# MoE expert slots without a token: their rows neither gathered nor stored, skipped by row numbers past a bound, and the result table filled with zeros earlier

## The chip, the cores and the metric

The kernel runs on one core of one Trainium2 chip. A core has a matrix engine (TensorE, PE in the profile, its weight loads PEld), a vector engine (DVE), a scalar engine (ACT), a general engine (GpSimd, POOL) and a sync engine (SP), which mostly issues transfers. Each engine works through its own instructions in order and waits on semaphores. SP, ACT and POOL each issue DMA transfers to queues of their own; 16 DMA engines carry them. The metric is the device time of one execution in microseconds.

## The reference, cut to what matters

One step of a one-layer decoder on 1088 tokens (1024 of a prompt, 64 of a sample group): a projection, an RWKV recurrence and a windowed attention, an output projection, a mixture of experts, a per-layer embedding and a last norm. The change lies in the mixture of experts:

```python
gsel = argmax(hf @ w_group + b_group)                  # one of 4 groups
tv, ti = top_k(elog[gsel], 2)                          # two of its 8 experts
tw = softmax(tv) * gw
for e in range(32):                                    # D = 1024, width of an expert 256
    out = (silu(hf @ w_gate[e]) * (hf @ w_up[e])) @ w_down[e]
    acc += comb[:, e, None] * out                      # comb is 0 but for the two chosen
```

Each token goes to two experts, so 1088 x 2 = 2176 rows are needed in all.

## The kernel before

The program has six phases. Phase 1 (to about 395 us) projects all tokens with `w_in`, one column tile `ct` at a time (25 of them), in 3 chunks of tokens, on PE; while it runs, SP writes its results to DRAM and copies the key and value caches. Phases 2 and 3 (to about 950 us) are the recurrence and the attention, phase 4 (to about 1079 us) is the output projection and the routing, phase 5 (to about 1420 us) the experts, phase 6 the embedding and the last norm.

Routing gives each of the 32 experts a list of `CAP` = 96 slots, 3072 in all. `idx[slot, expert]` is the number of the token in a slot; it comes out of a matrix product (`pidx`), so an empty slot holds 0, the number of token 0. `slot[token, 0..1]` is the row of a token's two results in the table `YE` (3072 x 1024 floats, in DRAM). With the reference's inputs no expert gets more than 96 tokens, so 2176 of the 3072 slots are used and 896 (29%) are empty.

Phase 5 does for each expert e:

- `gather(e)`: an indirect DMA on POOL's queue (L1532) fetches 96 rows of 4 KB from `HN` (the normed tokens) into `x5`. There are three buffers for x5, so gather e needs that PE is done with the x5 of expert e-3. It is asked for in round e-3.
- `xt(e)`: 8 PE transposes (L1542), and a split of the result in a high and a low part (ACT writes the high one, L47, DVE the low one, L49).
- `gu(e)`: 24 matmuls (128 x 512) with the gate and up weights, `act(e)` the gating, `ht(e)` two transposes.
- `down(e)`: 12 matmuls, evacuated by ACT in two halves into `y5` (L1575, three buffers, so y5 of expert e needs that the store of expert e-3 has landed), then a plain DMA on ACT's queue (L1576) that stores all 96 rows to rows 96e to 96e+95 of `YE`.

The weights of each expert (3.1 MB) are fetched by SP three rounds (gate, up) and five rounds (down) ahead, and split by ACT and DVE into high and low parts. In round 25 stands an `If` (L1647) on the largest count of an expert, with a path for full experts that isn't taken here. Phase 6 adds the two results of each token by indirect gathers of `YE` on POOL (L1712).

The order of the instructions of each engine isn't that of the source: a scheduler that keeps a simulated time line places them, all six phases together, so an edit in one place can move instructions elsewhere.

## Time and profile before

| | us |
|---|---|
| three runs | 1567.76, 1574.98, 1576.21 (median 1574.98) |
| the profiled execution | 1571.74 |
| its span, first to last instruction | 1570.0 |
| PE busy in the span | 1382.5 (88%) |
| DVE, ACT, POOL busy | 960.4, 738.1, 369.8 |
| experts, first transpose to last store's issue | 1079 to 1420 |

The busy shares are means over phases that are limited by different things. In the rows further down, a DMA share of 1.00 means that all 16 engines were busy all the time; values a little above come from the way in which packets are counted. "PEclk" is the clock granted to PE, 1.00 being full speed.

### The profile page before, as it was taken

How to read it: one execution, taken by the hardware profiler on the slowest of the kernel's cores; microseconds unless marked ns; L12 is line 12 of the kernel's file. 1: busy time of each engine (PE TensorE's matmuls, PEld its weight loads, DVE VectorE, ACT ScalarE, POOL GpSimd, SP SyncE). 2: the span in 40 equal slices, each digit the busy share in tenths (PEclk: the TensorE clock that was granted, in tenths of full speed). 3: DMA queues.
4: the chain of work that ended last, by engine and by line, in shares of the span. 5: the costliest groups of instructions: out<-in, count | busy, mean ns of one | idle time of the engine just before them, and what ended most of it. 6: DMA issues, size and time to landing. Idle time of an engine off the chain costs nothing. (4 is left out here: it accounts for less than half of the span.)

```text
span 1570.0 us, 24571 instructions
## 1 busy us (share of the span) xinstructions
PE 1382.5 (88%) x9017; PEld 1152.6 (73%) x9018; DVE 960.4 (61%) x2155; ACT 738.1 (47%) x1336; POOL 369.8 (24%) x362
## 2 busy tenths in 40 slices
PE   4899999999898998975679899995999789899996
PEld 4888999999777776754568678784777566567874
DVE  7524573462287686444457563567988678786664
ACT  5544453221334444522345463243878668783322
POOL 8104453000122223242122351112221101002231
PEclk9999999999898999987889899997999989999998
DMA  6145658896775675255586647558999999997552
GB/s 207 52 156 177 181 154 262 288 353 222 218 216 150 176 190 154 69 120 142 128 255 214 171 128 258 198 212 272 377 391 381 378 332 332 353 379 251 181 173 67
DMA packets 257005, 350.01 MB, mean 223 GB/s; under 512 B 105757, under 2 KB 184415, under 8 KB 256352
## 3 DMA queue, kind: packets, MB, share of 16 engines
q1 hardware_dynamic: 212272, 287.46, 56.0%
q0 software_dynamic: 39712, 43.76, 9.9%
q10 hardware_dynamic: 4896, 17.17, 2.9%
q8 instruction: 73, 1.20, 0.3%
q14 instruction: 52, 0.43, 0.1%
HBM read 277.45 MB, written 104.33 MB: 243 GB/s over the span
## 5 line engine op out<-in xcount | busy, mean ns | idle before, releaser
L264 PE MATMUL pj<-hT_hi,wh 128*128 128x384 f32 (+1 forms) x600 | 199.5, 334 | 4.7 <-DVE lora L272 2.7
L264 PE MATMUL pj<-hT_hi,wl 128*128 128x384 f32 (+1 forms) x600 | 199.1, 332 | 0.0
L264 PE MATMUL pj<-hT_lo,wh 128*128 128x384 f32 (+1 forms) x600 | 198.4, 331 | 0.0
L264 PEld LDWEIGHTS pj<-hT_hi,wh 128*128 128x128 f32 x600 | 114.0, 191 | 6.6 <-DVE lora L272 3.0
L264 PEld LDWEIGHTS pj<-hT_hi,wl 128*128 128x128 f32 x600 | 114.0, 190 | 2.4 <-issue 2.2
L264 PEld LDWEIGHTS pj<-hT_lo,wh 128*128 128x128 f32 x600 | 114.4, 191 | 0.6 <-issue 0.2
L1532 POOL DMA_INDIRECT x<-HN,idx x32 | 49.9, 1560 | 255.2 <-PE p4t L1542 154.1
L49 DVE TENSOR_TENSOR dl<-draw,dh 128x1024 fp32r<-128x1024 f32 x66 | 78.0, 1221 | 43.8 <-ACT dh L47 43.6
L1040 PE MATMUL pS<-k,q 128*128 128x512 f32 (+2 forms) x192 | 55.7, 397 | 37.9 <-DMA q<-QP 36.5
L688 DVE TENSOR_TENSOR ftmp<-At,X 128x60 f32<-128x60 f32 (+24 forms) x248 | 59.7, 252 | 44.1 <-DMA At<-ABd 33.5
L1069 PEld LDWEIGHTS po<-v,pt 128*128 128x128 f32 x576 | 74.5, 198 | 11.0 <-issue 2.7
L1069 PE MATMUL po<-v,pt 128*128 128x128 f32 x576 | 80.0, 284 | 1.6 <-ACT pt L1067 1.3
L1052 ACT ACTIVATE s<-s,nm 128x128 f32<-128x128 f32 (+7 forms) x64 | 49.4, 772 | 62.7 <-DVE X L744 21.5
L47 ACT ACTIVATE dh<-draw 128x1024 fp32r<-128x1024 f32 x66 | 66.2, 1052 | 22.9 <-DMA draw<-in_w_down_dram 13.5
L1040 PEld LDWEIGHTS pS<-k,q 128*128 128x128 f32 x192 | 32.2, 206 | 44.2 <-issue 31.9
L1043 DVE CUSTOM_DVE_ANT_0 s<-pS,bias 128x512 f32<-128x512 f32 (+2 forms) x96 | 50.8, 551 | 19.5 <-PE pxt L1063 15.9
L49 DVE TENSOR_TENSOR wl<-w,wh 128x1024 fp32r<-128x1024 f32 x25 | 35.0, 1400 | 44.6 <-ACT wh L47 43.8
L690 DVE TENSOR_TENSOR X<-X,ftmp 128x60 f32<-128x60 f32 (+24 forms) x248 | 58.7, 248 | 4.5
L1067 ACT ACTIVATE pt<-pxt 128x512 f32<-128x512 f32 (+3 forms) x64 | 32.6, 512 | 58.9 <-PE pxt L1063 44.1
L767 POOL TENSOR_TENSOR s<-S,pc 128x512 f32<-128x512 f32 x16 | 16.9, 1055 | 161.9 <-PE pj L264 70.6
L1289 PE MATMUL p4y<-dh,hh 128*96 128x512 f32 x128 | 46.9, 407 | 7.5 <-ACT hh L47 7.5
L1289 PE MATMUL p4y<-dh,hl 128*96 128x512 f32 x128 | 51.3, 401 | 1.3 <-DVE hl L49 1.3
(653 smaller groups left out, 3793.4 us busy)
## 6 DMA issues: line engine op xcount, KB each, us to landing
wraw<-in_w_gate_dram SPq DMA_DIRECT2D x64, 512.0 KB
wraw<-in_w_up_dram SPq DMA_DIRECT2D x64, 512.0 KB
draw<-in_w_down_dram SPq DMA_DIRECT2D x32, 1024.0 KB
out_dram<-in_cache_k_win_dram SPq DMA_DIRECT2D x16, 1016.0 KB
out_dram<-in_cache_v_win_dram SPq DMA_DIRECT2D x16, 1016.0 KB
w<-in_w_in_dram SPq DMA_DIRECT2D x25, 512.0 KB
kc<-in_cache_k_win_dram SPq DMA_DIRECT2D x48, 256.0 KB
vc<-in_cache_v_win_dram SPq DMA_DIRECT2D x48, 256.0 KB
```

Of the source, the lines that this page charges most:

```text
L47: (hi_eng or nc.scalar).activation(hi, src, AF.Copy) if (hi_eng or nc.scalar) is nc.scalar else hi_eng.tensor_copy(hi, src)
L49: return e.tensor_tensor(lo, src, hi.bitcast(F32), op=ALU.subtract)
L264: nc.tensor.matmul(p[:, :nn], a[:, k, :], b[:, k, n0:n0 + nn], start=(m == 0), stop=(m == 23))
L688: nc.vector.tensor_tensor(o, At[:, t, t + 1:32][:, :, None].to_broadcast([128, m, c]), X[:, t, None, 0:c].to_broadcast([128, m, c]), op=AL ...
L690: nc.vector.tensor_tensor(X[:, t + 1:32, 0:c], X[:, t + 1:32, 0:c], o, op=ALU.add)
L1040: nc.tensor.matmul(ps[:, :n], q[:, a, i * 128:(i + 1) * 128], k[:, c0:c0 + n], start=(a == 0), stop=(a == 1))
L1043: nc.vector.tensor_tensor_reduce(s[:, c0:c0 + n], ps[:, :n], bias[:, bo:bo + n], 1.0, -3e38, ALU.add, ALU.max, m)
L1052: ex = nc.scalar.activation(s[:, :nb * 128], s[:, :nb * 128], AF.Exp, bias=nm, accum_out=den)
L1067: nc.scalar.activation(pt[:, b0:b0 + m, :], px[:, :m, :], AF.Copy)
L1069: nc.tensor.matmul(po, pt[:, b, :], v[:, b, :], start=(b == 0), stop=(b == nb - 1))
L1289: self.nc.tensor.matmul(p, a[x][:, k, :], w, start=(k == 0 and q == 0), stop=(k == kn - 1 and q == 2))
L1532: nc.gpsimd.indirect_dma_start(out=X[e][:n], out_offset=None, in_=self.HN, in_offset=bass.IndirectOffsetOnAxis(ap=self.idx[:, e:e + 1], ax ...
```

## The change

`idx` gets 2048 added, and the table of token numbers from which it is made has 2048 taken off: a used slot holds its token's number as before, an empty one 2048. The gather gets a bound, the last token (1087): rows whose number is above are skipped. A second index `row[slot, expert]` holds the slot's row in `YE`, plus 4096 where the slot is empty. The store becomes an indirect DMA on POOL's queue with this index and the bound 3071, again with skipping. `YE` is filled with zeros in phase 1 by 12 DMAs of 1 MB on SP, one for each of the projections number 8 to 19 (`n`), each with a declared wait for the evacuation of that projection's first chunk.

```diff
@@ project
+            if n0 == 0 and 8 <= n < 20:
+                z = nc.sync.dma_start(self.YE[256 * (n - 8):256 * (n - 7), :].rearrange("(p a) (b c) -> p (a b) c", a=2, c=512),
+                                      self.S0.rearrange("p i v -> p (i v)")[:, None, :].to_broadcast([128, 4, 512]))
+                self.tc.add_manual_dep(z.ins, a.ins.name, ...)
@@ constants
+FREE = 2048
-    row[:, 140:149] = j[:, None] + 128 * np.array(ORD)[None, :]
+    row[:, 140:149] = j[:, None] + 128 * np.array(ORD)[None, :] - FREE
+    row[:, 149] = j
@@ phase4_
-        self.after_idx = nc.vector.tensor_copy(self.idx, pidx[:CAP, 0:NE])
+        nc.vector.tensor_scalar(self.idx, pidx[:CAP, 0:NE], float(FREE), None, op0=ALU.add)
+        free = p4.tile([CAP, NE], F32, name="free")
+        nc.vector.tensor_scalar(free, pidx[:CAP, 0:NE], 0.0, float(2 * FREE), op0=ALU.is_ge, op1=ALU.mult)
+        nc.vector.scalar_tensor_tensor(self.row, free, row[:CAP], ist[:CAP], op0=ALU.add, op1=ALU.add)
@@ gather
             nc.gpsimd.indirect_dma_start(out=X[e][:n], out_offset=None, in_=self.HN,
-                                         in_offset=bass.IndirectOffsetOnAxis(ap=self.idx[:, e:e + 1], axis=0))
+                                         in_offset=bass.IndirectOffsetOnAxis(ap=self.idx[:, e:e + 1], axis=0),
+                                         bounds_check=T - 1, oob_is_err=False)
@@ down
-            return nc.scalar.dma_start(self.YE[e * n:e * n + n, :], y[:n])
+            return nc.gpsimd.indirect_dma_start(out=self.YE, out_offset=bass.IndirectOffsetOnAxis(ap=self.row[:, e:e + 1], axis=0),
+                                                in_=y[:n], in_offset=None, bounds_check=NE * CAP - 1, oob_is_err=False)
```

Before, the stores of two experts write different rows by their addresses, and nothing orders them. An indirect store may write any row of `YE` as far as the program can tell, so each one waits until the one before it has landed, and the first `y6` gather of phase 6 waits for the last.

The order of instructions changes on every engine. On POOL, before, the gathers of phase 5 stand one behind the other (here those of experts 15 to 20; the number behind a name is its buffer's):

```order
L1532 DMA x5_12321<-HN_88,idx_9885 96x1024
L1532 DMA x5_12423<-HN_88,idx_9885 96x1024
L1532 DMA x5_12525<-HN_88,idx_9885 96x1024
L1532 DMA x5_12627<-HN_88,idx_9885 96x1024
L1532 DMA x5_12729<-HN_88,idx_9885 96x1024
```

Now, just ahead of the `If`, the gathers of experts 27 and 28 (x5_13661, x5_13767) and the stores of experts 14 to 24 (y5_12719 to y5_13779) stand like this:

```order
L1588 DMA YE_89<-y5_12719,row_9898 3072x1024
L1543 DMA x5_13661<-HN_88,idx_9897 96x1024
L1588 DMA YE_89<-y5_12825,row_9898 3072x1024
L1543 DMA x5_13767<-HN_88,idx_9897 96x1024
L1588 DMA YE_89<-y5_12931,row_9898 3072x1024
L1588 DMA YE_89<-y5_13037,row_9898 3072x1024
...
L1588 DMA YE_89<-y5_13673,row_9898 3072x1024
L1588 DMA YE_89<-y5_13779,row_9898 3072x1024
L1659 TENSOR_LOAD ci_13812
```

POOL has now 32 stores between its gathers. Behind gather 28 stand nine stores in a row (experts 16 to 24), behind the `If` gathers 29 and 30, store 25, gather 31, the stores 26 to 31, and then the first gather of phase 6.

On ACT, before, the two evacuations of expert 24 and its store's issue are all that stands of down in the stretch ahead of the `If`, with splits of weights between them:

```order
L1575 ACTIVATE y5_13657<-p4y_13658 96x512
L47 ACTIVATE dh_13679<-draw_13277 128x1024 x2
L1575 ACTIVATE y5_13657<-p4y_13666 96x512
L47 ACTIVATE wha_13653<-wraw_13486 128x1024
L47 ACTIVATE wha_13675<-wraw_13486 128x1024
L1576 DMA YE_89<-y5_13657 96x1024
L47 ACTIVATE whb_14208<-wraw_13585 128x1024
L47 ACTIVATE whb_14212<-wraw_13585 128x1024
L1646 TENSOR_LOAD ci_13688
```

Now the evacuations of experts 21 to 24 (y5_13461, y5_13567, y5_13673, y5_13779) come there close together:

```order
L1587 ACTIVATE y5_13461<-p4y_13470 96x512
L1587 ACTIVATE y5_13567<-p4y_13568 96x512
L47 ACTIVATE dh_13591<-draw_13173 128x1024 x2
L1587 ACTIVATE y5_13567<-p4y_13576 96x512
...
L1587 ACTIVATE y5_13673<-p4y_13674 96x512
L47 ACTIVATE dh_13697<-draw_13279 128x1024 x2
L1587 ACTIVATE y5_13673<-p4y_13682 96x512
...
L1587 ACTIVATE y5_13779<-p4y_13780 96x512
L47 ACTIVATE dh_13803<-draw_13385 128x1024 x2
L1587 ACTIVATE y5_13779<-p4y_13788 96x512
L1659 TENSOR_LOAD ci_13812
```

On PE the downs have moved likewise: from about expert 9 on they fall behind the gate and up products, to five experts behind (the down of expert 19 stands in the gate and up of expert 23), and those of 19 to 24 stand in the last rounds ahead of the `If`.

On SP, in phase 1, before, a row of cache copies, stores and weight loads:

```order
L596 DMA bb0_99<-BB_70 64x4x64 x4
L281 DMA out_8_dram<-in_cache_k_win_dram 16x16256
L281 DMA out_9_dram<-in_cache_v_win_dram 16x16256
L297 DMA QP_76<-qhi_2523 128x1024
L608 DMA AR_2216<-ARd_68 128x4x256
L608 DMA AR_2322<-ARd_68 128x4x256
```

Now the zero fills (L277) stand among them, two in this stretch:

```order
L600 DMA bb0_99<-BB_70 64x4x64 x4
L277 DMA YE_89<-S0_109 512x1x512
L285 DMA out_8_dram<-in_cache_k_win_dram 16x16256
L285 DMA out_9_dram<-in_cache_v_win_dram 16x16256
L612 DMA AR_2222<-ARd_68 128x4x256
L612 DMA AR_2328<-ARd_68 128x4x256
L301 DMA QP_76<-qhi_2530 128x1024
L301 DMA QP_76<-qlo_2531 128x1024
L302 DMA QT_78<-qk_2442 128x64
L277 DMA YE_89<-S0_109 512x1x512
L235 DMA w_2823<-in_w_in_dram 128x8x128
```

A weight load `w` that stands behind a zero fill is issued only after it.

## Rows read from the trace of the kernel before

**Rows 1.** The page: span, busy time of the engines, data rate in 40 slices.
```profile
span 1570.0 us, 24571 instructions
PE 1382.5 (88%) x9017; PEld 1152.6 (73%) x9018; DVE 960.4 (61%) x2155; ACT 738.1 (47%) x1336; POOL 369.8 (24%) x362
GB/s 207 52 156 177 181 154 262 288 353 222 218 216 150 176 190 154 69 120 142 128 255 214 171 128 258 198 212 272 377 391 381 378 332 332 353 379 251 181 173 67
```

**Rows 2.** Windows of phase 5: busy us of each engine, then PEclk, DMA share, GB/s.
```profile
core 0: us, PE busy (x) PEld busy (x) DVE busy (x) ACT busy (x) POOL busy (x), PEclk, DMA share, GB/s
1100.00:1166.00 66.00, 66.00 (x333) 47.35 (x332) 61.52 (x78) 55.20 (x82) 17.80 (x7) 1.00 1.03 382
1166.00:1318.00 152.00, 136.77 (x648) 94.93 (x647) 119.34 (x151) 111.23 (x166) 18.96 (x15) 0.94 0.99 356
1352.00:1424.00 72.00, 67.55 (x320) 48.55 (x318) 58.30 (x72) 54.45 (x80) 3.18 (x4) 0.96 0.88 333
```

**Rows 3.** Timeline of POOL, gathers of experts 9, 10, 14 and 28: start, us.
```profile
1121.39 2.86 POOL L1532 DMA_INDIRECT x<-HN,idx  x1 [6.29 <-PE p4t L1542]
1130.53 2.86 POOL L1532 DMA_INDIRECT x<-HN,idx  x1 [6.29 <-PE p4t L1542]
...
1166.64 0.91 POOL L1532 DMA_INDIRECT x<-HN,idx  x1 [7.63 <-PE p4t L1542]
...
1318.30 2.17 POOL L1532 DMA_INDIRECT x<-HN,idx  x1 [2.09 <-PE p4t L1542]
```

**Rows 4.** DMA queues, 1105 to 1225 us: packets, MB, share; gathers' landing.
```profile
q1 hardware_dynamic: 9696, 36.03, 77.8%
q0 software_dynamic: 1504, 5.31, 13.9%
q10 hardware_dynamic: 1456, 5.11, 10.7%
...
x<-HN,idx POOLq DMA_INDIRECT x14, 9.2
```

**Rows 5.** The same view, 960 to 1065 us: POOL's queue, stores to DRAM only.
```profile
q0 software_dynamic: 2096, 7.60, 18.5%
...
HN<-hn POOLq DMA_DIRECT2D x8, 512.0 KB, 6.8
X<-x POOLq DMA_DIRECT2D x7, 512.0 KB, 5.8
```

**Rows 6.** Tile x: all 32 gathers, ns min, median, max on POOL.
```profile
L1532 POOL DMA_INDIRECT x<-HN,idx x32: 905/1021/3158, 1072.6 to 1369.0; - x32
```

**Rows 7.** Timeline of the end of phase 5: last store, first gather of phase 6, its reader.
```profile
1420.13 0.31 ACTq L1576 DMA_DIRECT2D YE<-y  x1
...
1423.98 0.98 POOL L1712 DMA_INDIRECT y<-YE,slot  x1 [54.02 <-DMA PL<-ple]
...
1429.03 1.28 DVE L1721 SCALAR_TENSOR_TENSOR x<-y,wgt,x 128x1024 f32<-128x1024 f32 x1 [1.48 <-DMA y<-YE,slot]
...
1442.63 1.04 PE L1736 MATMUL p4t<-ident,hp 128*128 128x128 f32 x8
```

**Rows 8.** Phase 1: two windows, columns as in rows 2.
```profile
200.00:300.00 100.00, 98.55 (x621) 97.73 (x620) 46.76 (x44) 39.38 (x69) 31.50 (x23) 1.00 0.72 229
300.00:400.00 100.00, 97.31 (x608) 96.38 (x607) 45.49 (x157) 21.69 (x41) 0.88 (x2) 0.98 0.82 278
```

**Rows 9.** DMA queues, 200 to 260 us, then 260 to 330 us.
```profile
q1 hardware_dynamic: 17217, 10.81, 61.0%
...
q1 hardware_dynamic: 14481, 21.76, 90.0%
```

**Rows 10.** Timeline of the start of phase 5.
```profile
1071.53 0.17 DVE L1484 CAST idx<-p4g 96x32 int32<-96x32 f32 x1
...
1079.11 1.54 PE L1542 MATMUL p4t<-ident,x 96*128 96x96 f32 x8 [7.82 <-DMA x<-HN,idx]
```

More of the change, by code (lines that the diff above doesn't have):

```diff
@@ L271, in project @@
                     nc.scalar.activation(self.sh[:, :, ct], p[:, o:o + 65:8], AF.Copy)
-                nc.vector.scalar_tensor_tensor(out[:, n0:n0 + nn], p[:, :nn], self.omu[:, ct:ct + 1],
+                a = nc.vector.scalar_tensor_tensor(out[:, n0:n0 + nn], p[:, :nn], self.omu[:, ct:ct + 1],
                                                tmp[:, n0:n0 + nn], op0=ALU.mult, op1=ALU.add)
@@ L275, in project @@
                 a = nc.scalar.activation(out[:, n0:n0 + nn], p[:, :nn], AF.Copy, scale=0.125 if ct < 17 else 1.0)
+            if n0 == 0 and 8 <= n < 20:
+                z = nc.sync.dma_start(self.YE[256 * (n - 8):256 * (n - 7), :].rearrange("(p a) (b c) -> p (a b) c", a=2, c=512),
+                                      self.S0.rearrange("p i v -> p (i v)")[:, None, :].to_broadcast([128, 4, 512]))
+                self.tc.add_manual_dep(z.ins, a.ins.name, mybir.DependencyInfo(mybir.DependencyClass.Sync, mybir.DependencyReason.DATA))
         return a if ct >= 13 else None
@@ L1305, in phase4_ @@
         self.idx = c4.tile([CAP, NE], I32, name="idx")
+        self.row = c4.tile([CAP, NE], I32, name="row")
         xs_p = I['x_prompt'].rearrange("o t d -> (o t) d")
@@ L1315, in phase4_ @@
         i4, i8, ist = rc[:, 128:132], rc[:, 132:140], rc[:, 140:172]
-        irk, tid = rc[:, 172:172 + CAP], rc[:, 268:277]
+        irk, tid, row = rc[:, 172:172 + CAP], rc[:, 268:277], rc[:, 277:278]
         ones = p4.tile([128, 128], F16, name="ones")
```

## The prediction

> **What bounds the kernel now.** I read the page first, then cut the span into phases by windows, then asked in phase 5 for the pace of the experts and for the DMA queues. On the page PE is busy 88% of the span [rows 1], so one could take it for the bound everywhere; but the data rate reaches its highest values, 330 to 390 GB/s, in slices 29 to 36, which are phase 5. The windows of that phase [rows 2] show two regimes. From 1100 to 1166 us PE is busy all of the time while the DMA engines are full (1.03): weights are still ahead from phase 4. From 1166 to 1318 us PE is busy for 136.8 of 152 us, DVE for 119 and ACT for 111, and the DMA share stays at 0.99: nothing on the compute engines is full, the DMA engines are. The gathers of POOL give the pace, since one is asked for per expert [rows 3]: 9.14 us apart at 1121 to 1130 us, the pace of a full PE; from expert 14's at 1166.64 to expert 28's at 1318.30 it is 151.7 / 14 = 10.83 us per expert, the pace of the DMA engines. So bytes taken out of phase 5 are worth time for about 20 experts, down to a floor of PE's 9.14 us.
>
> **What a row costs.** In 1105 to 1225 us, 120 us, the queues' shares give the price of a MB in time of all 16 engines [rows 4]: weights 0.778 x 120 / 36.03 = 2.59 us, gathers (POOL's queue) 0.139 x 120 / 5.31 = 3.14 us, stores (ACT's queue) 0.107 x 120 / 5.11 = 2.51 us. POOL's queue with stores alone, from 960 to 1065 us, gives 0.185 x 105 / 7.60 = 2.56 us [rows 5]; I take that for the new stores, and keep 3.14 us, the price of the gathers, for the other end.
>
> **The gain.** Per expert a gather moves 96 x 4 KB = 0.393 MB, and 29% of it goes: 0.115 MB x 3.14 = 0.36 us. The store was 0.393 MB x 2.51 = 0.99 us and becomes 0.279 MB x 2.56 = 0.71 us, 0.27 us less (by the other price 0.88, 0.11 us less). Together 0.63 us (0.47) per expert, 10.83 to 10.20 us; PE's floor isn't reached. Experts 12 to 31 are at the DMA pace: 20 x 0.63 = 12.6 us. The earlier ones run at PE's pace with the DMA engines full, so what they save lets weights arrive sooner and moves the change of regime back: at most 12 x 0.63 = 7.6 us more. I take a little of that, 14 us, and 9 (20 x 0.47) to 20 us as the bounds. This supposes that a skipped row makes no transfer. No row here shows a skipped one; the bound on the other side is no gain at all.
>
> **The chain of stores.** The stores were independent. Now each waits for the landing of the one before; behind a waiting store on POOL stand the gathers, whose landing PE's transposes await, and y5 of expert e waits for store e-3, which holds ACT, and behind ACT the PSUM buffers and PE. Call c the time of one link, from issue to landing. In steady state a round has one store and one gather, c + 0.9 to 3.2 us of issue [rows 6] in 10.2 us, which fits up to c = 7 to 9. The order shown in the part on the change makes it worse at the end: between gather 28 and the first gather of phase 6 stand the stores 16 to 31, sixteen links. Gather 28 was issued at 1318.30 [rows 3], the first gather of phase 6 at 1423.98 [rows 7], 105.7 us. The experts in it give back some 3 us, and PE's next work on the result begins at 1442.63 without a wait, of which I count 2 us as slack: 16c = 105, c = 6.6. Since the transposes of expert 25 now stand two rounds ahead of the `If`, gather 28 can be issued up to a round earlier: 16c = 115, c = 7.2. Up to about 6.9 the chain costs little; above it 16 us for each us of c if nothing gives, which I lower to 12, as some of it overlaps with waits for weights.
>
> What is c? Stores of 512 KB on this queue landed in 6.8 and 5.8 us where it was less full [rows 5]; gathers of 384 KB in 9.2 us in the full stretch [rows 4]. The new stores move 279 KB on average: scaled with bytes 9.2 x 0.71 = 6.5, not scaled 9.2, and at the least some 5, below the quicker of the two stores. I take 6.5, near the gather of the same stage, and with it a cost of 3 us (y5 and POOL's issue time take some slack); c = 5 costs nothing, c = 7.5 about 7, c = 9.2 about 28 us.
>
> The stores leave ACT's queue for POOL's, and the rows show that POOL is slow at times: the same gather took 0.91 or 3.16 us of it [rows 6], and 2.86 us in each of the rounds at 1121 to 1130 [rows 3]. The Trainium skill, page "SBUF — State Buffer" (summary of rules and the box on the DVE trap), says that descriptors of a DMA issued on GpSimd can't be written while DVE holds the port that they share, and advises to issue such a DMA from ACT or SP: exactly the reverse of this edit. By that rule every link would be longer by what the slow gathers took, 3.16 - 0.91 = 2.2 us, so c about 8.7 and the chain some 20 us instead of 3; the median of rows 6, 1.02 us, makes it the exception. Another rule speaks for the change: page "DMA: Bandwidth & Descriptors" (anatomy of one DMA) gives 2.0 us plus bytes at 436 GB/s, an estimate of 2.6 us for 279 KB and no cost of the chain at all, 1560 us; the same formula gives 3.2 us for 512 KB, where rows 5 have 5.8 to 6.8, so here the rows decide.
>
> **The zero fill.** 12 x 1.05 = 12.6 MB more in phase 1, at 2.59 us per MB 33 us of the DMA engines, between about 160 and 330 us. PE is busy there for 98.6 and 97.3 of 100 us [rows 8], and the share of the weights' queue, which does all of it, is 61% from 200 to 260 us and 90% from 260 to 330 [rows 9]: some 23 us are free in the first stretch and 7 in the second, and more ahead of and behind both. So most of it fits, but a weight load that stands behind a fill on SP, or the reads of the recurrence at the end, come later. PE's own waits are only 1.4 and 2.7 us now, which says that the loads have reserve. Nothing at the least, 8 us (a quarter of the 33) at the most; I take 2.
>
> **The rest.** Two more small DVE operations and one longer one at the start, 0.17 us each as the cast of idx [rows 10], in front of the first gather or beside it; PE waits 7.82 us for that gather. 0.3 us. ACT loses an issue of 0.31 us per expert [rows 7], off the path. The other phases are reordered by the scheduler with no work added; I count nothing, with 6 us either way.
>
> **The sum** is made against the profiled execution's own 1571.74 us, 3.2 below the median of 1574.98 and inside the three runs: 1571.7 - 14 + 3 + 2 + 0.3 = 1563.0 us. Differences within 0.5%, 7.9 us, can't be told from none with this kernel.
>
> **The rivals.**
> *The gain is given back.* The chain runs at c = 7.2 to 8, above its threshold, or the downs that stand together ahead of the `If` wait for y5: 4 to 12 us more than I count, 1567 to 1577. For it: c lies close under the threshold by my own estimate, and 9.2 us is a row of the very stage. Against: fewer rows, and a DMA stage that is itself relieved.
> *The skip saves nothing.* A skipped row still makes a transfer, or the stage is limited by packets of weights rather than by these bytes; then the gain is 0 and the costs stay: 1571.7 + 3 + 2 + 0.3 = 1577. For it: no row shows a skip. Against: a price per MB that comes from the same queues.
> *Slower: POOL's stores are the bound.* One mechanism: c of 8.5 us, by issues of 3.16 us on POOL instead of 1.02 [rows 6] or by landing like a gather's. Sixteen links take 136 us where 105 to 115 are there; by 12 us above 6.9 it is 19 us, by 16 it is 26: 1563 - 3 + 19 = 1579 to 1586 us. It decides from c = 7.7, where it passes the gain. A sign of it would be PE waiting ahead of the `If` for ACT's evacuation, and POOL's first gather of phase 6 late.
> *The fill delays phase 1.* 8 us instead of 2, with c as forecast: 1569.
> *More gain.* The savings of the early experts count in full and c is 5: 1571.7 - 20 + 2 + 0.3 = 1554.
>
> **Chances.** The forecast (1557 to 1567) 0.37; more gain 0.07; the gain given back 0.20; skip without saving 0.06; fill 0.06; slower by POOL's stores 0.24. Set against 1574.98, with 0.5% from 1567.1 to 1582.9: faster are the forecast and more gain, 0.44; the same are those given back, without saving, the fill, 0.32 together; the slower case ends above that bound for c over 8.3 and up to 9.2 us (1591), and with all its weight there 0.24. The range leaves out most of more gain and the worst of the slower case: 1553 to 1588. The likeliest case alone is 1557 to 1567.
>
> **What the profile after would show.** The gathers' spacing between experts 14 and 28 falls to about 10.2 us; if it stays at 10.8, the skip or the stage was misjudged. The DMA bytes of phase 5 fall by 7.3 MB, those of phase 1 rise by 12.6. The stores of POOL stand one landing apart wherever they are late: their spacing between 16 and 24 is c itself, 6 to 7 us. PE's wait at the `If` doesn't grow, and the first gather of phase 6 comes within some 2 us of the last expert's end. PE's idle time in 200 to 400 us stays below 6 us. The prediction is wrong if c is above 7.5, if the fills stand in front of loads that PE awaits, or if the new order of other phases costs more than 6 us.

## The result, and the profile after

The changed kernel takes 1634.97 us (median of 4 runs, 1631.34 to 1644.14) against 1571.37 us before (4 runs, 1567.47 to 1576.21): a ratio of 1.042, 95% interval 1.039 to 1.046. The forecast was 1563. The profiled execution took 1631.34 us, its span is 1629.6 us, 59.6 us longer than the span of before. Runs of one kernel scatter by some 5 us (standard deviation), and two executions further down, of 7325 and 3359 us, were slow ones that the ratios leave out.

The page of the changed kernel, the lines that answer to [rows 1], and its DMA queues:

```profile
span 1629.6 us, 24772 instructions
PE 1405.4 (86%) x9017; PEld 1167.4 (72%) x9018; DVE 963.8 (59%) x2157; ACT 739.8 (45%) x1336; POOL 407.0 (25%) x394
...
GB/s 199 62 167 191 241 227 294 322 343 240 236 193 128 175 145 168 82 140 91 136 223 218 237 91 230 194 245 247 357 366 340 351 341 245 300 297 225 196 172 65
...
q1 hardware_dynamic: 218608, 300.04, 56.8%
q0 software_dynamic: 43296, 49.01, 10.4%
q10 hardware_dynamic: 1312, 4.59, 0.8%
```

The bytes moved as the change says: on the page of before the three queues carried 287.46, 43.76 and 17.17 MB, so SP's queue (q1) got 12.58 MB of zeros, ACT's (q10) lost the stores' 12.58 MB, and POOL's (q0) has 5.25 MB more, 8.92 of stores less 3.67 of skipped gathers. No slice of the experts (from slice 29 on) stays near 380 GB/s any more, and one falls to 245.

Where the time went is seen by four moments of each trace, and the stages between them are what the whole document goes by: the end of the last projection, the issue of the first gather of the experts on POOL, the first gather of the results, the end of the span.

| us | last projection starts its last product | first gather of the experts | from there to the first gather of the results | from there to the end |
|---|---|---|---|---|
| before | 399.3 | 1072.6 | 351.4 | 146.0 |
| after | 413.7 | 1104.7 | 379.5 | 145.4 |

So 32 us are lost ahead of the experts, where the change adds the zero fill and a few small operations on the indices, and 28 us in the experts, where it takes bytes away. The last phase is as before. Within the experts the loss lies at the end: from the first gather to that of expert 28 it is 242.9 us, before 245.7, and from there to the first gather of the results 136.6 us, before 105.7. The gathers' pace improves as forecast, from 10.1 to 9.6 us between experts 13 and 28, and says nothing of the time.

The timeline of POOL in the changed kernel (start, us, instruction, idle time before it and what ended it), from the gather of expert 28 over the stores 16 to 24 to the gather of expert 29, which stands behind the `If`, and then the first gather of the results:

```profile
1347.66 0.98 POOL L1543 DMA_INDIRECT x<-HN,idx  x1 [5.34 <-PE p4t L1554]
1348.95 0.92 POOL L1588 DMA_INDIRECT YE<-y,row  x1 [0.30 <-issue]
1354.93 1.20 POOL L1588 DMA_INDIRECT YE<-y,row  x1 [5.06 <-DMA YE<-y,row]
1360.78 0.91 POOL L1588 DMA_INDIRECT YE<-y,row  x1 [4.65 <-ACT h L1567]
1369.73 0.91 POOL L1588 DMA_INDIRECT YE<-y,row  x1 [8.04 <-ACT y L1587]
...
1405.10 0.91 POOL L1588 DMA_INDIRECT YE<-y,row  x1 [3.69 <-DMA YE<-y,row]
1406.93 0.97 POOL L1543 DMA_INDIRECT x<-HN,idx  x1 [0.91 <-DMA draw<-in_w_down_dram]
...
1484.21 0.99 POOL L1725 DMA_INDIRECT y<-YE,slot  x1 [3.77 <-PE p4y L1295]
```

The stores 16 to 24 go out from 1348.95 to 1405.10 us, 56.2 us for eight links, 7.0 us each. In five of the eight (the stores 17, 18, 22, 23 and 24) the store goes out 0.75 or 0.76 us behind the landing of the one before it, its own data being ready; these links are 4.8 to 8.4 us long. The list of waits names the landing for only two of them (4.8 and 6.0 us) and for the others work of ACT on tiles that the store doesn't touch. The other three stores, and all of the seven behind the `If`, wait for the evacuation of their own expert. From gather 28 to gather 29 it is 59.3 us; before it was 35.1, from 1318.30 [rows 3] to 1353.38. Windows of the same kernel (columns as in [rows 2]), for the experts up to 13, the stores' run ahead of the `If`, and the rest:

```profile
1104.00:1213.00 109.00, 98.36 (x478) 70.44 (x478) 91.00 (x122) 79.61 (x117) 33.02 (x22) 0.92 0.92 323
...
1348.00:1407.00 59.00, 46.83 (x183) 30.82 (x182) 36.98 (x44) 37.04 (x54) 10.84 (x11) 0.89 0.75 257
1407.00:1484.00 77.00, 69.64 (x314) 49.60 (x313) 56.06 (x70) 52.78 (x78) 13.01 (x10) 0.91 0.76 258
```

The DMA share falls to 0.75 there: waits, and no longer bytes, set the pace. PE is idle for 12 of 59 us, and its granted clock is 0.89, so its products take longer too. PE's own waits in the experts of the changed kernel (us in total, times, longest):

```profile
PE p4y L1295 <- ACT hh L47: 9.6, 5, 2.6
PE p4t L1554 <- DMA x<-HN,idx: 8.2, 1, 8.2
PE p4g L1295 <- DVE h L1569: 5.1, 3, 2.6
PE p4t L1554 <- DVE xl L49: 5.0, 3, 2.3
```

None of these names a store. A store could be behind them: ACT may not evacuate expert e into `y5` before the store of expert e-3 has landed, and the splits that PE waits for (`hh`) stand behind the evacuations on ACT. In this trace that isn't seen: no evacuation begins less than 2.6 us after the landing that it needs, and the one that begins at 1396.61 us (expert 24) needs store 21, which landed at 1392.00. What is seen is PE and ACT waiting for each other in turn over the late downs that the order crowds together there: PE (the first line) for a split `hh` that stands behind a split of weights and an evacuation on ACT, and ACT (the other lines) for PE's next products:

```profile
1393.37 0.70 PE L1295 MATMUL p4y<-dh,hh 128*96 128x512 f32 x2 [2.39 <-ACT hh L47]
...
1390.61 2.00 ACT L47 ACTIVATE dh<-draw 128x1024 fp32r<-128x1024 f32 x2 [0.29 <-PE p4y L1295]
1392.52 0.57 ACT L1587 ACTIVATE y<-p4y 96x512 f32<-96x512 f32 x1
1393.00 0.31 ACT L47 ACTIVATE hh<-p4h 128x192 fp32r<-128x192 f32 x1
1393.21 0.37 ACT L1567 ACTIVATE h<-p4g 96x256 f32<-96x256 f32 x1
1396.61 0.59 ACT L1587 ACTIVATE y<-p4y 96x512 f32<-96x512 f32 x1 [3.02 <-issue]
1398.31 2.00 ACT L47 ACTIVATE dh<-draw 128x1024 fp32r<-128x1024 f32 x2 [1.11 <-PE p4y L1295]
1400.22 0.57 ACT L1587 ACTIVATE y<-p4y 96x512 f32<-96x512 f32 x1
1406.63 0.33 ACT L47 ACTIVATE hh<-p4h 128x192 fp32r<-128x192 f32 x1 [5.83 <-PE p4h L1577]
```

### The profile page after: what moved, and what is told of

Same layout as the page of the kernel before. It is cut to its first block, busy times and chain, and to the rows that moved or that the text cites. A ratio compares the mean times of both kernels' runs of the same rounds, so it can differ in the third digit from the quotient of the medians.

```text
span 1629.6 us, 24772 instructions
## 1 busy us (share of the span) xinstructions
PE 1405.4 (86%) x9017; PEld 1167.4 (72%) x9018; DVE 963.8 (59%) x2157; ACT 739.8 (45%) x1336; POOL 407.0 (25%) x394
## 5 line engine op out<-in xcount | busy, mean ns | idle before, releaser
L692 DVE TENSOR_TENSOR ftmp<-At,X 128x54 f32<-128x54 f32 (+24 forms) x248 | 61.0, 254 | 51.3 <-DMA At<-ABd 36.3
L1588 POOL DMA_INDIRECT YE<-y,row x32 | 42.3, 1322 | 140.8 <-ACT y L1587 66.2
L1295 PE MATMUL p4y<-dh,hh 128*96 128x512 f32 x128 | 52.9, 436 | 12.3 <-ACT hh L47 9.6
L694 DVE TENSOR_TENSOR X<-X,ftmp 128x54 f32<-128x54 f32 (+24 forms) x248 | 59.9, 251 | 5.0
```

Of the source, the lines that this page charges most:

```text
L692: nc.vector.tensor_tensor(o, At[:, t, t + 1:32][:, :, None].to_broadcast([128, m, c]), X[:, t, None, 0:c].to_broadcast([128, m, c]), op=AL ...
L694: nc.vector.tensor_tensor(X[:, t + 1:32, 0:c], X[:, t + 1:32, 0:c], o, op=ALU.add)
L1295: self.nc.tensor.matmul(p, a[x][:, k, :], w, start=(k == 0 and q == 0), stop=(k == kn - 1 and q == 2))
L1588: return nc.gpsimd.indirect_dma_start(out=self.YE, out_offset=bass.IndirectOffsetOnAxis(ap=self.row[:, e:e + 1], axis=0), in_=y[:n], in_of ...
```

## The experiments

All ratios are to the kernel before, from runs on the same chip, with 95% intervals. "Experts" is the time from the first gather of the experts to the first gather of the results, "ahead" the time up to the former, both from the profiled execution. That is one execution of each kernel, and "ahead" is the less certain of the two: PE's instruction list up to the experts is the same in the kernel before and in seven of the kernels below (those without a fill, but for the one with the late first loads), and "ahead" lies between 1070.5 and 1081.1 us in these eight. Where the list of the experts is the same as well, "experts" agrees within 1 us (351.4 and 350.7; 360.6 and 361.5). First the parts of the change one at a time.

**The fill alone.** The twelve fills are added to the kernel before, nothing else.

```diff
+            if n0 == 0 and 8 <= n < 20:
+                z = nc.sync.dma_start(self.YE[256 * (n - 8):256 * (n - 7), :]..., self.S0...)
+                self.tc.add_manual_dep(z.ins, a.ins.name, ...)
```

> The kernel before with the twelve zero fills alone; gathers and stores are as before. Theory A (the fill costs the time ahead of the experts): the first gather of the experts comes at 1095 to 1107 us instead of 1072.6, the experts take 345 to 355 us as before, and the whole is 25 to 35 us slower than before. Rival B (any edit makes the scheduler reorder phases 1 to 4, and the fill itself fits into free transfer time): first gather at 1070 to 1080 us, whole within 8 us of before.

1610.62 us, ratio 1.025 (1.021 to 1.029); ahead 1107.3 us, experts 351.7: theory A, a little past the ends of its ranges. The loss ahead of the experts comes with the fill, all of it, and the experts lose nothing by it.

**The gather's skip alone.** No fill, the store plain on ACT's queue as before; the indices are made as in the change.

```diff
+                                         bounds_check=T - 1, oob_is_err=False)
...
             return nc.scalar.dma_start(self.YE[e * n:e * n + n, :], y[:n])
```

> The kernel before with the skipping gathers alone (indices with 2048 added, bound on the gather); the stores stay plain transfers on ACT's queue, no fill. If skipped rows save transfer time where DMA paces the experts, 3 to 8 us faster than before. Rival B: the first gather comes 10 us or more later than at 1072.6 us, by reordering. If the skip saves bytes and no time: within 3 us.

1580.93 us, ratio 1.006 (1.003 to 1.009); ahead 1080.4 us, experts 360.4. None of the three expectations: by the interval the kernel is 4 to 14 us slower. The order of PE's instructions up to the experts is that of before, in the experts it isn't. The bytes were saved. From the first gather of the experts to that of the results (packets, MB, share), 350.9 us in the trace of before:

```profile
DMA packets 35582, 124.09 MB, mean 354 GB/s; under 512 B 3504, under 2 KB 4592, under 8 KB 35554
...
q0 software_dynamic: 3584, 12.58, 11.6%
```

and 359.6 us with the skip:

```profile
DMA packets 35548, 120.29 MB, mean 335 GB/s; under 512 B 4400, under 2 KB 5488, under 8 KB 35519
...
q0 software_dynamic: 3584, 8.92, 8.1%
```

A gather takes 0.116 x 350.9 / 32 = 1.27 us of the 16 engines before, and 0.081 x 359.6 / 32 = 0.91 us with the skip. The saving of 0.36 us per gather is that of the prediction; the stage did not get shorter by it. The number of packets on POOL's queue is the same, 3584: 896 more of all packets are under 512 bytes, one for each empty slot.

**The chain alone.** Stores as indirect DMAs of all 96 rows on POOL's queue; no skipping and no fill.

```diff
-            return nc.scalar.dma_start(self.YE[e * n:e * n + n, :], y[:n])
+            return nc.gpsimd.indirect_dma_start(out=self.YE, out_offset=bass.IndirectOffsetOnAxis(ap=self.row[:, e:e + 1], axis=0),
+                                                in_=y[:n], in_offset=None, bounds_check=NE * CAP - 1, oob_is_err=False)
```

> The kernel before with the stores as indirect transfers on POOL's queue, all 96 rows each, so nothing is skipped and nothing is filled. Theory C (the chain of stores, each waiting for the landing of the one before, costs phase 5 its time): first gather of the experts near 1073 us, from there to the first gather of the results 375 to 390 us instead of 351, whole 25 to 40 us slower than before. Rival D (the loss of phase 5 comes from the later start of the experts, with their weights' prefetch and order changed by the fill): 345 to 358 us, whole within 8 us.

1606.34 us, ratio 1.019 (1.014 to 1.024); ahead 1081.1 us, experts 385.2, 33.8 more than before. Here the waits of ACT name the landing of a store outright, so that the link over `y5` does occur in this kernel (us, times, longest):

```profile
ACT y L1579 <- DMA YE<-y,row: 8.0, 6, 3.4
```

**The change with four tables.** Expert e stores to table e mod 4, so the false dependence reaches only to the store of expert e-4.

```diff
-        self.YE = d.tile([NE * CAP, D], F32, name="YE")
+        self.YE = [d.tile([NE * CAP // 4, D], F32, name="YE%d" % k) for k in range(4)]
...
+            return nc.gpsimd.indirect_dma_start(out=self.YE[e % 4], ...)
...
+                d = nc.gpsimd.indirect_dma_start(out=y[:n], out_offset=None, in_=self.YE[3], ...)
```

> The changed kernel with the results in four tables, expert e's in table e mod 4, so that a store waits for the store of expert e-4 only; fill, skipping and POOL's issues are kept. Phase 6 reads all rows from the fourth table, so its sums are not those of the reference. Theory C: from the first gather of the experts to that of the results 340 to 352 us instead of 379.5, whole 1600 to 1610 us. Rival D: 370 to 382 us, whole 1625 to 1640 us.

1615.97 us, ratio 1.027 (1.023 to 1.031); ahead 1106.8 us, experts 355.9, near theory C and 4 us above its range. POOL's issues, the skipping and the fill are all there, and 23.6 of the 28 us are gone. POOL's stores now wait for ACT alone, no landing stands in the list:

```profile
POOL YE L1588 <- ACT y L1587: 104.7, 18, 8.6
POOL YE L1588 <- ACT hh L47: 47.3, 13, 9.9
POOL YE L1588 <- ACT h L1567: 5.0, 1, 5.0
```

So 23.6 of the 28 us come with the false dependence. But a link of 6 to 7 us should fit into a round of 10. In the kernels with one table the instruction list of PE has the downs of the experts from about 12 to 22 three to four experts behind their gate and up, instead of one to two with four tables or before. That gave the next question: do the links cost the time, or the order that the scheduler makes in reckoning with them?

**The chain in the order of the source.** The kernel of the chain alone, with the products of the experts held in program order, so the down of an expert stands one behind.

```diff
                 i = self.nc.tensor.matmul(p, a[x][:, k, :], w, ...)
+                if getattr(self, 'pin', 0):
+                    self.tc.keep_in_program_order(i)
```

> The kernel of the chain alone (indirect stores of all rows, nothing skipped, nothing filled), with the gate, up and down products of the experts held in the order of the source, so that the down of an expert stands one expert behind instead of three or four. Theory C (the links' own time): the chain binds again, 375 to 385 us from the first gather of the experts to that of the results. Rival E (the scheduler, which reckons with slow links, puts the downs three to four experts late, and that order costs the time; the real links of 6 to 7 us fit into a round): 350 to 360 us, and whole within 10 us of before.

1590.14 us, ratio 1.013 (1.009 to 1.016); experts 367.0. **The same order without the chain**, as a measure:

> The kernel before with the same products held in the order of the source, stores plain on ACT's queue: the measure for the run above. If one expert of lag is enough: 348 to 356 us from first gather to first gather, whole within 5 us of before. If the slack of two experts was needed: 5 to 20 us slower.

1567.57 us, ratio 0.997 (0.994 to 0.999); experts 349.4. This is the only kernel with the full result here whose interval lies below 1, by little. So of the 33.8 us of the chain alone, 18.2 go with the late downs, and 17.6 (367.0 less 349.4) are left to the chain with the downs in place; by the medians of the whole, on two chips, it is 15 and 23 us. Neither theory had it alone. What is left isn't the links' time alone: only the products are held, and the transposes on PE and the work of ACT, DVE and SP stand in another order with the chain than without.

**The fill elsewhere.** The same twelve fills from rounds 2 to 7 of the recurrence instead of the projections, and then in the projections on POOL's queue.

```diff
+            if u >= 2:
+                n = 2 * u + c - 4
+                z = nc.sync.dma_start(self.YE[256 * n:256 * (n + 1), :]..., self.S0...)
```

> The kernel before with the twelve zero fills alone, but issued in rounds 2 to 7 of the recurrence (after 470 us) instead of in the projections. Theory F (the fill costs what the transfer engines and SP's issue lack in the stage where it stands): the share of the engines is 0.45 to 0.62 from 500 to 700 us, so 0 to 15 us slower than before, against 39 in the projections. Rival G (12.6 MB cost their 33 us wherever they stand, because loads behind them wait): 25 to 40 us.

1576.78 us, ratio 1.003 (1.001 to 1.005); ahead 1069.4 us, experts 360.6: theory F, and what is lost is lost in the experts, whose order has changed.

```diff
-                z = nc.sync.dma_start(self.YE...
+                z = nc.gpsimd.dma_start(self.YE...
```

> The kernel before with the twelve zero fills alone, in the projections as in the change, but issued on POOL's queue. If SP's queue was the point (loads stand behind a fill in SP's order): 0 to 15 us slower than before. If it is the transfer engines' time in that stage: 25 to 40 us, as with SP.

1625.22 us, ratio 1.032 (1.028 to 1.037); the last projection starts its last product at 419.9 us, ahead 1122.7. That is above both ranges: SP's queue was not the point, POOL's makes it some 12 us worse by the ratios, and the place decides.

**The gather's skip in the order of the source.** The skip alone, beside the same order without it.

> The skipping gathers alone, as in the run of the gather skip, with the products of the experts held in the order of the source; to be set beside the source order alone (349.4 us from the first gather of the experts to that of the results, whole 1567.6). Theory H (the bytes pace the experts): 343 to 347 us, whole 1560 to 1564. Rival I (the share of the transfer engines is full because loads wait in it, and their pace comes from the buffers that ACT, DVE and PE free): 347 to 353 us, whole 1564 to 1572.

1577.97 us, ratio 1.004 (1.002 to 1.007); experts 356.7 against 349.4. Neither theory allowed for more than 353. By the ratios, 1.004 against 0.997, the skip makes this order some 12 us slower. The gather of expert 28 comes as far behind the first as without the skip (245.7 and 244.6 us), but between it and the gather of expert 29, behind the `If`, 42.2 us pass instead of 33.3. The products stand in the same order in both, the rest of PE's list and those of ACT, DVE and SP don't; what in them does it was not followed up.

**Fewer bytes, without skip, chain or fill.** 68 of the 96 rows are gathered and stored; then 64, when 68 turned out to land late.

```diff
+SL = 68
-            nc.gpsimd.indirect_dma_start(out=X[e][:n], ...idx[:, e:e + 1]
+            nc.gpsimd.indirect_dma_start(out=X[e][:SL], ...idx[:SL, e:e + 1]
-            return nc.scalar.dma_start(self.YE[e * n:e * n + n, :], y[:n])
+            return nc.scalar.dma_start(self.YE[e * SL:e * SL + SL, :], y[:SL])
```

> What the bytes are worth with no chain, no fill and no skipping: gathers and plain stores of 68 of the 96 rows of each expert (the mean use), products in the order of the source; slots 68 to 95 are left out, so their tokens' results are not those of the reference. Theory H: 0.63 us less for each of 20 to 30 experts, 331 to 339 us instead of 349.4, whole 1549 to 1557. Rival I: 344 to 351 us, whole 1562 to 1570.

1627.33 us, ratio 1.036 (1.032 to 1.039), experts 409.9: far from both. POOL's queue from the first gather of the experts to that of the results, all queues' packets, and the landing of a gather:

```profile
DMA packets 39908, 116.67 MB, mean 285 GB/s; under 512 B 9648, under 2 KB 10736, under 8 KB 39880
...
q0 software_dynamic: 9216, 8.94, 9.5%
...
x<-HN,idx POOLq DMA_INDIRECT x32, 11.8
```

These are 288 packets per gather instead of 112 with 96 rows, and they land in 11.8 us instead of 8.0. The rows are still packets of 4 KB: their 8.94 MB are 2176 of them, and packets of 512 bytes to 2 KB are no more than before (1088). What has come are some 220 packets under 512 bytes per gather instead of 16; the next expectation has them as packets of 1 KB, which is only their mean. The run tests another thing than was meant.

> Gathers and plain stores of 64 of the 96 rows of each expert (68 rows, tried before, came out as packets of 1 KB, which 64 rows should not), products in the order of the source; slots 64 to 95 are left out, so their tokens' results are not those of the reference. To be set beside the source order alone, 349.4 us and 1567.6. Theory H (bytes pace the experts; 0.131 MB less per gather and per store, 0.74 us per expert): 328 to 338 us, whole 1546 to 1557. Rival I (buffers and the compute engines pace them): 344 to 351 us, whole 1562 to 1570.

1567.60 us, ratio 0.996 (0.993 to 0.999); experts 342.5, 6.9 less than with all rows and the products in the same order. 0.131 MB less in each of 32 gathers and stores is 8.4 MB, more than the 7.3 that the change takes from the experts. At the prices of the prediction 20 of 0.74 us would be 15 us. Less than half of that came, nearer to the rival; and the whole did not become measurably shorter than in the run with the source order alone (1567.57): in the execution profiled "ahead" was 7.7 us longer (1079.9). Yet bytes do count for something here: in 152 us of the stage SP's queue carried 46.00 MB of weights instead of 44.05, with the DMA share at 1.01 and 0.99. With the gather's skip it carried them as fast as before, 0.28 MB a us, with a share of 0.95 instead of 0.99.

**Where the fill's 35 us arise.** First the place of attention's first loads, which the kernels with a fill in the projections issue behind the recurrence's last work on POOL:

```diff
+        self.tc.add_manual_dep(d.ins, self.last_s.ins.name, ...)      # d: the load of k in head()
```

> The kernel before with one thing moved: the loads of the first two attention heads' k wait on POOL for the last scaling of the recurrence's state, which is where the order of the kernels with a fill in the projections has them. Theory J (that place is worth about 11 of the 35 us that these kernels lose ahead of the experts): attention's first product comes 15 to 18 us behind the recurrence's last instead of 6.4, whole 6 to 12 us slower. Rival K (the fill's transfers, not the order, make it late): 6 to 8 us, whole within 4 us.

1585.05 us, ratio 1.008 (1.005 to 1.010). Attention's first product starts 14.7 us behind the last product of the recurrence with its state (before 6.4), about as theory J has it, but ahead is 1073.7 us: the attention gives it back. The 13 us are lost elsewhere, 10 of them in the experts (361.5), whose instruction list on PE here is that of the run with the fill in the recurrence (360.6), and neither is that of before. So theory J's price fails for what this run moves. It moves less than was meant: k is asked for at 683.9 us instead of 675.6, and PE's order there hardly changes; in the kernel with the half of the fill, which follows, k and q are asked for from 695.8 us on. Then the size of the fill, a quarter and a half:

```diff
-  self.YE[256 * (n - 8):256 * (n - 7), :]
+  self.YE[256 * (n - 8):256 * (n - 8) + 64, :]      # the quarter; + 128 for the half
```

> The kernel before with the twelve fills in the projections, each a quarter as long (64 rows instead of 256, 3.1 MB in all). With these the scheduler leaves the recurrence, the attention and the experts in the order of before. Theory L (the transfers' own time costs what the fill costs, in proportion): a quarter of 35, 8 to 10 us more until the first gather of the experts, whole 8 to 10 us slower. Rival M (the new order of the later phases costs most of it): 0 to 4 us.

1570.68 us, ratio 1.000 (0.997 to 1.004); ahead 1066.4 us, experts 350.7.

> The same with 128 rows in each fill, 6.3 MB in all; here the scheduler turns the order of recurrence and attention over as with the whole fill. Theory L: 16 to 20 us slower. Rival M: 20 to 30 us, a jump from the quarter to the half.

1600.44 us, ratio 1.016 (1.009 to 1.023); ahead 1106.8 us, experts 352.6. The half costs as much ahead of the experts as the whole, as rival M has it. Windows of 200 to 300 and 300 to 400 us, of the quarter

```profile
200.00:300.00 100.00, 98.62 (x618) 98.08 (x617) 44.12 (x43) 37.06 (x64) 27.93 (x19) 1.00 0.76 240
300.00:400.00 100.00, 94.89 (x585) 93.63 (x585) 48.94 (x157) 21.71 (x40) 0.40 (x1) 0.97 0.83 279
```

of the half

```profile
200.00:300.00 100.00, 98.62 (x618) 98.08 (x617) 42.06 (x43) 37.32 (x65) 26.76 (x18) 1.00 0.76 248
300.00:400.00 100.00, 95.24 (x592) 93.74 (x591) 49.45 (x156) 21.75 (x40) 0.40 (x1) 0.98 0.83 290
```

and of the whole fill:

```profile
200.00:300.00 100.00, 98.11 (x607) 97.15 (x606) 41.15 (x42) 37.28 (x61) 28.82 (x19) 1.00 0.84 279
300.00:400.00 100.00, 88.62 (x538) 87.09 (x537) 48.64 (x156) 22.42 (x40) 0.40 (x1) 0.93 0.93 318
```

Quarter and half can't be told apart in the stage in which the fills are carried, PE is as busy and the DMA share the same; the half's last fill is issued at 328.7 us and its last projection starts its last product at 401.3 us, the quarter's at 403.0. The first gather of the experts is 40 us apart in the executions profiled, which are the fastest of the quarter and the slowest of the half; the medians of the whole are 30 us apart. What differs is the instruction lists: with the quarter PE's list of recurrence, attention and all that follows is that of before, with the half some 850 of its rows from the recurrence to the routing stand elsewhere. The traces show where the time goes. Before, attention's first product stands amid the recurrence's last (PE's timeline):

```profile
688.51 0.45 PE L1040 MATMUL pS<-k,q 128*128 128x128 f32 x1 [6.17 <-DMA q<-QP]
...
697.20 0.65 PE L789 MATMUL wy<-u,LAB 128*64 128x128 f32 x4
```

With the half it stands behind them all, and PE idles for 12 us until its q has landed:

```profile
701.98 0.65 PE L793 MATMUL wy<-u,LAB 128*64 128x128 f32 x4
714.68 0.45 PE L1044 MATMUL pS<-k,q 128*128 128x128 f32 x1 [12.04 <-DMA q<-QP]
```

Attention's last product starts at 950.8 us before, at 947.7 with the quarter, 989.3 with the half and 989.9 with the whole: all of the loss is there by then, 26 of the half's 38 us at attention's first product and the rest in the attention itself. From 700 to 1060 us PE is busy for 307 and 310 us before and with the quarter, 290 and 291 with the half and the whole, and its granted clock is 0.92 and 0.94 there against 0.87 and 0.88.

**All together, mended.** The whole change with the fill in the recurrence and the products in source order, and the fill there with the source order alone.

> The whole change with two mendings: the zero fill in rounds 2 to 7 of the recurrence, and the products of the experts in the order of the source; skipping gathers, skipping stores and their chain as in the change. If the parts add up (fill there 4.6, chain in this order 16 to 18, source order -4.6, skipping 0 to -6): 1578 to 1592 us, experts 355 to 367 us. If the parts don't add up, the fill in the recurrence moves other work again: over 1600.

1580.44 us, ratio 1.006 (1.003 to 1.009), experts 361.8: the parts add up as well as the intervals let one see, and the change so mended is some 54 us better than as made, and still not faster than before.

> The fill in the recurrence, with the products of the experts in the order of the source, to be set beside the source order alone (1567.6). If the fill costs nothing in the recurrence and the 10 us of the experts in the run of the fill in the recurrence came from their order: experts 348 to 353 us, whole 1564 to 1572. If the fill's transfers cost there: 1573 to 1585.

1577.23 us, ratio 1.003 (0.999 to 1.006); ahead 1063.7 us, experts 357.9. Nothing is lost ahead of the experts; the experts take 8.5 us more than in source order without a fill, with another order of the work around the products. The expectation that the fill costs nothing is missed: beside the source order alone, 1.003 (0.999 to 1.006) against 0.997 (0.994 to 0.999), it costs some 9 us, though not where its transfers are.

## Why the prediction was wrong

**What failed first: "I count nothing, with 6 us either way" for the other phases.** With the term of the fill (2 us, 8 at the most) it was to stand for all that happens ahead of the experts, where the fill alone costs 35 us; beside it stand the chain, 34 us for 3, and the gain, none for 14. In the projections the fill already passes its bound of 8 us: PE in 300 to 400 us is busy for 88.6 us with the whole fill instead of 97.3 [rows 8], and the last projection ends some 13 us later; PE's idle time in 200 to 400 us, which was to stay below 6, is 14.9 us in the changed kernel. The half adds 2 us there, the quarter 4. But ahead of the experts the half and the whole both lose 34 to 35 us, and the quarter, which leaves the later order as it was, loses nothing. So for the half it is the order of the recurrence and the attention that costs it: its fills have long been carried, and the lists are what differs from the quarter then. The whole fill has nearly the half's order there, so the same is argued for it; but 13 of its 35 us could be the transfers', with the order's share smaller, and no run has the whole fill in the projections with the order of before. Which of the moved rows do it is open. The late first loads of the attention were tried by themselves, 12 us less late than with the half, and cost nothing ahead of the experts; attention's start behind the recurrence's last products, as with the half, was not tried.

**The chain: the link was right, the way of summing it wrong.** c was taken as 6.5 us; the stores 16 to 31 landed after 6.2 us in the mean and 6.8 in the median, those from 1213 to 1348 us after 8.1. The step that failed is "up to about 6.9 the chain costs little". It set sixteen links of c against the time of the work, as if the links ran beside the work. They took 1484.21 - 1348.95 = 135.3 us, 8.5 each, because they alternate with it: five of them are held by the landing before, and go out 0.76 us behind it, for which the sum had nothing; the others wait for their evacuation, which the late downs bring late. And about half of the cost is not the links but the order made for them, 18.2 of 33.8 us by the experts' time. The order on record in the part on the change shows these late downs and the nine stores in a row; the prediction used them to place the links and gave the lateness itself no price.

**The gain: right in bytes, wrong in time.** The engines' time saved per gather is the forecast 0.36 us, yet 14 us did not appear. The two runs with less to move in the same order of products give 7 us less in the experts (64 rows) and 7 us more (the skip); of the whole, nothing that can be told and some 12 us more. The prediction took a DMA share of 0.99 as the bound of the stage [rows 2]. In the run with the gather's skip the share is 0.95, and the stage is no shorter: there the engines' time is not what the next expert waits for. With 64 rows it is in part, since the weights come 4% faster at a full share. That the loads wait for buffers that ACT, DVE and PE free would fit the skip's run, but is not shown, and as the order around the products changed in both, the price of a byte alone stays open. Part of the error is plain counting: the gather at 1166.64 us [rows 3] is that of expert 13, not 14, so the pace there is 151.7 / 15 = 10.11 us and not 10.83, one us above PE's 9.14 and not 1.7. (The other numbers in the label of that group are one too high in the same way for the gathers at 1121 and 1130.)

**The chances.** The rival in which POOL's stores are the bound was right in place and direction, at 0.24. Its sum of sixteen links, 136 us, is what was measured, 135.3, but by luck: a link of 8.5 us was to come from slow issue or landing, and the landings are 6.2 us in the mean, the issue 1.29 us in the median. Its sign, PE waiting ahead of the `If` for ACT's evacuation, is there for 2.7 us in all; PE waits longer for ACT's splits. It came to 1579 to 1586 because it kept the gain and the fill's 2 us. (In its upper end, 1591 for c = 9.2, the 3 us of the forecast's chain are counted twice: by 12 us for each us of c it is 1588, by 16 it is 1597.) The rival of the fill was priced at 8 us, a quarter of what the fill cost. On the rule of the Trainium skill against issuing on GpSimd (page "SBUF — State Buffer", summary of rules): the four tables keep all 32 issues on POOL and cost 4.5 us in the experts, so here it was not what decided. And the estimate by the Trainium skill's page "DMA: Bandwidth & Descriptors" (anatomy of one DMA), 2.6 us for such a store, is below every landing of such a store in the changed kernel: 3.6 us at the least, 6.8 in the median of the emptier stretch.

## What to carry to other kernels

A transfer whose address comes from data is, for the program, a write to the whole table: count not only its bytes but the wait that each one now has for the last, the time between a landing and the next issue, and the order that a scheduler makes in reckoning with it. Where a scheduler orders the whole program, the price of an edit includes the orders that it turns over elsewhere; compare the instruction lists of the untouched phases first, and shrink the edit to see at which size the order flips and whether the time goes with it. And a full share of the DMA engines is no proof that every byte saved comes back as time: take bytes away without anything else, hold the order of all engines, not of the products alone, and see what comes back.

## What the runs showed of the hardware that was not expected

A row that an indirect DMA skips by its bound moves no data but still shows as a packet: over the 32 gathers of the experts the packets on POOL's queue stayed at 3584 while the bytes fell from 12.58 to 8.92 MB, and the packets under 512 bytes of all queues rose from 3504 to 4400, by one for each of the 896 empty slots. The engines' time fell by 0.36 us per gather all the same.

The number of rows of an indirect gather changes how it is carried: 96 rows of 4 KB came as 112 packets and landed in 8.0 us, 64 rows as 80 packets in 7.5 us (2560 packets for 32 gathers), but 68 rows as 288 packets in 11.8 us. The surplus is of packets under 512 bytes, 220 per gather instead of 16, and the engines' time per gather is no longer (1.21 us against 1.25 for 96 rows, by 9.5% of 409.2 us and 11.5% of 348.8 us); the landing is. With 68 rows the experts took 60 us longer than with 96 rows in the same order of products (409.9 against 349.4).

A store that waits for nothing but the landing of the one before it on POOL went out 0.75 to 0.78 us behind that landing, in the eight cases of the changed kernel (the stores 3, 13, 15, 17, 18, 22, 23 and 24).
